# Layer 1's query stage with VectorE in written order, and the scaling of the queries behind the sums of both halves

## The chip, the core and the metric

The kernel runs on one core of one Trainium2 chip. The metric is the device time of one execution in microseconds; lower is better. The time before is 1675.03 us, the median of three runs (1675.02 to 1677.68).

The profile calls the engines PE (TensorE, the matmuls; PEld is its weight load), DVE (VectorE), ACT (ScalarE), POOL (GpSimd) and SP (SyncE, which issues nearly all DMAs here).

## What is computed

Two layers of a transformer-like backbone over 1024 latent tokens and 256 context tokens, model width 1024, fp32. Layer 0 is grouped-query attention, layer 1 multi-head latent attention with 16 heads. Only layer 1's queries matter here. Cut to them, the reference is:

```python
def q_heads(q_a, n):
    q = (rms_norm(q_a, p["q_a_norm"]) @ p["w_q_b"]).reshape(B, n, 16, 64 + 32)
    q = rms_norm(q, p["q_norm"])
    return jnp.split(q, [64], axis=-1)

kv_a, k_r, q_a, g = jnp.split(h @ p["w_in"], cuts, axis=-1)   # q_a: 384 columns, g: 1024
q_nope, q_rope = q_heads(q_a, S)
q_rope = apply_axial_rope(q_rope, cos, sin)
...
y = (o.reshape(B, S, 1024) * jax.nn.silu(g)) @ p["w_out"]
```

So each token's 384 query latents are normalised, expanded to 16 heads of 96, normalised per head, and the last 32 of each head are rotated.

## The kernel before

**Precision by splitting.** Every fp32 matrix operand is held as two parts, a high one (`wa`, `hh`, `qah`, `th`) and the rest (`wb`, `hl`, `qal`, `tl`). ACT copies out the high part, DVE or POOL subtracts it from the source (`split` in line 87 and 88; the weights in lines 158 and 137). A product is three matmuls: high by high, high by low, low by high (`mm3`, lines 94 to 96).

**The query stage.** It goes over 8 tiles of 128 tokens, in two passes. Its steps for a tile:

- `q_compress`: 24 matmuls against the input projection (384 columns), the sum of squares on ACT (L1733), the root (`rstd_of`: a multiply-add on DVE in L118, a power on POOL in L120), the scaled latents `qan` on DVE (L1736). First pass only.
- `q_latent`: three transposes on PE, the split into `qah` and `qal` (L87, L88), and their store to DRAM for the second pass (there `q_fetch` loads them).
- `q_expand`: 8 heads per pass, worked on in two halves of 4 heads (`q4`). A half is 9 matmuls of 128x384 into an `mm` buffer of PSUM, the squares on ACT (L1768), and then on DVE the sum per head (`qss`, L1770), the multiply-add of the root (`q_ms`, L118), the products with the gain and cosine table (`t`, L1775) and with the gain and sine table (two instructions `qt`, L1780). POOL takes the power (`q_rs`, L120) and adds `qt` into `t` (L1782). Last, DVE scales `t` by the root (L1783).
- `gate`: in some tiles a slice of the gate projection, 24 matmuls of 128x512, a tanh on ACT (L305) and a product on DVE (`gth`, L306), stored by SP.
- `q_store`: for each half three transposes on PE into a `tp` buffer (L1793), the split into `th` and `tl` (L87, L88), and two stores on SP (`q1h`, `q1l`, L1798).

There are four `mm` buffers and four `tp` buffers in PSUM. The tiles `th` and `tl` have two buffers each. Squares, products and gate slices share eight buffers in SBUF (tag `w512`).

**The order of the work.** `staged` writes the steps skewed: in round t it writes compress of tile t, latents of t - 1, expand of t - 3, the gate slice that belongs to t - 4, and the store of t - 6 (second pass: fetch of t, expand of t - 1, gate of t - 2, store of t - 3). The written order is not the order that runs. The framework puts each engine's instructions in an order at build time, by estimates of its own, and may take a later instruction ahead of an earlier one. Inside `with in_order(engine)` (line 82, which is the framework's manual schedule for one engine) that engine's instructions keep the written order. The key/value stage before has such a block for DVE (line 1621), and its `kv_expand` already holds the first half's scaling until the second half's sum is written. The query stage has none. The loads and splits of weights (`load_weight`, L137, L154, L158) are written before, between and behind the two passes, and stand in no block: between the passes the second half of the query expansion (`wqb`) and the second gate weight (`wg1`).

Behind the query stage come the other gate slices, and from the fifth of them on the attention's first row maxima (L402), whose operands `KH`, `QH` and `QR` SP loads from what the key/value and query stages stored.

Of the kernel before, what the change touches and what calls it, by code (L numbers as in the profile page):

```python
# [25 lines left out]
TL = NL // P  # L26
# [11 lines left out]
def hybrid_kernel(ctx: ExitStack, tc: tile.TileContext, ins: dict, out: bass.AP):  # L38
# [43 lines left out]
    def in_order(engine):  # L82

        return tc.manual_schedule(engines={engine})
# [5 lines left out]
    def mm3(ps, lh, ll, rh, rl, ks, first=True, last=True, between=None):  # L90

        ks = list(ks)
        for i, k in enumerate(ks):
            pe.matmul(ps, lhsT=lh(k), rhs=rh(k), start=first and i == 0, stop=False)  # L94
            pe.matmul(ps, lhsT=lh(k), rhs=rl(k), start=False, stop=False)  # L95
            pe.matmul(ps, lhsT=ll(k), rhs=rh(k), start=False, stop=last and i == len(ks) - 1)  # L96
            if between is not None:
                between(i)

    def staged(items, *stages):  # L100

        items = list(items)
        held = {}
        for t in range(len(items) + len(stages) - 1):
            for j, stage in enumerate(stages):
                i = t - j
                if 0 <= i < len(items):
                    held[i] = stage(items[i], held.get(i))
# [5 lines left out]
    def rstd_of(small, ss, n, tag):  # L114

        w = ss.shape[-1]
        ms = small.tile([P, w], F32, name=tag + "_ms", tag=tag + "_ms")
        dve.tensor_scalar(ms, ss, 1.0 / n, EPS, op0=ALU.mult, op1=ALU.add)  # L118
        rs = small.tile([P, w], F32, name=tag + "_rs", tag=tag + "_rs")
        pool.tensor_tensor(rs, ms, mhalf[:, :w], op=ALU.pow)  # L120
        return rs
# [17 lines left out]
    def load_weight(w, kt, c0, cols, share=2, slot=None, todo=None):  # L139
        a, b = slot or ring_pair()  # L140
        pitch = -(-cols // 64) * 64
        wh, wl = (t[:, : kt * pitch].rearrange("p (k n) -> p k n", n=pitch)[:, :, :cols] for t in (a, b))
        src = w[:, c0:c0 + cols].rearrange("(k p) n -> p k n", p=P)
        wid = min(cols, 1024)
        step = max(1, 1024 // cols)
        for k in range(0, kt, step):
            for c in range(0, cols, wid):
                n = min(step, kt - k)

                def piece(k=k, n=n, c=c):  # L150
                    r = rawp.tile([P, 1024], F32, name="wraw", tag="wraw")
                    rv = r[:, : n * wid].rearrange("p (k n) -> p k n", n=wid)
                    ks, cs = slice(k, k + n), slice(c, c + wid)
                    sp.dma_start(rv, src[:, ks, cs])  # L154

                    def parts(share=share):
                        for j in range(n):
                            act.copy(wh[:, k + j, cs], rv[:, j, :])  # L158
                            sub_any(wl[:, k + j, cs], rv[:, j, :], raw(wh[:, k + j, cs]), share)

                    return parts

                if todo is None:
                    piece()()
                else:
                    todo.append(piece)
        return wh, wl
# [126 lines left out]
    def gate_slice(l, c, m, s0, n, w, hT, ps_mm, wk, between={}):  # L294

        hh, hl = hT[0 if s0 < NL else 1]
        hs = slice(s0 % NL, s0 % NL + n)
        ms = slice(m * P, (m + 1) * P)
        ps = ps_mm.tile([P, 512], F32, name="mm", tag="mm")
        for k0 in range(0, KT, KT // 2):  # L300
            between.get(k0, lambda: None)()
            mm3(ps[:, :n], lambda k: w[0][:, k, ms], lambda k: w[1][:, k, ms],
                lambda k: hh[:, k, hs], lambda k: hl[:, k, hs], range(k0, k0 + KT // 2), k0 == 0, k0 + KT // 2 == KT)
        th = wk.tile([P, 512], F32, name="gth", tag="w512")
        act.activation(th[:, :n], ps[:, :n], AF.Tanh, scale=0.5)  # L305
        dve.scalar_tensor_tensor(th[:, :n], th[:, :n], 1.0, ps[:, :n], op0=ALU.add, op1=ALU.mult)  # L306
        sp.dma_start(sgd[l][4 * c + m, :, s0:s0 + n], th[:, :n])
# [1400 lines left out]
    with ExitStack() as st:  # L1708
# [49 lines left out]

        def q_expand(tt, c, w, lat):
            qah, qal = lat  # L1760
            held = []
            for q4 in range(2):
                ns = slice(384 * q4, 384 * q4 + 384)
                ps = ps_mm.tile([P, 512], F32, name="mm", tag="mm")
                mm3(ps[:, :384], lambda k: qah[:, k, :], lambda k: qal[:, k, :],
                    lambda k: w[0][:, k, ns], lambda k: w[1][:, k, ns], range(3))
                sq = wk.tile([P, 512], F32, name="sq", tag="w512")
                act.activation(sq[:, :384], ps[:, :384], AF.Square)  # L1768
                ss = small.tile([P, 4], F32, name="qss", tag="qss")
                dve.reduce_sum(ss, sq[:, :384].rearrange("p (h d) -> p h d", d=96), axis=AX.X)  # L1770
                rs = rstd_of(small, ss, 96, "q")
                pv = ps[:, :384].rearrange("p (h d) -> p h d", d=96)
                t1 = wk.tile([P, 512], F32, name="t1", tag="w512")
                t1v = t1[:, :384].rearrange("p (h d) -> p h d", d=96)
                dve.tensor_tensor(t1v, pv, cwq[:, tt, :].unsqueeze(1).broadcast_to([P, 4, 96]), op=ALU.mult)  # L1775
                t2 = small.tile([P, 4, 2, 2, 8], F32, name="qt2", tag="qt2")
                p5 = pv[:, :, 64:96].rearrange("p h (a s d) -> p h a s d", a=2, s=2)
                sv = swq[:, tt, :].rearrange("p (a s d) -> p a s d", a=2, s=2)
                for s_ in range(2):
                    dve.tensor_tensor(t2[:, :, :, s_, :], p5[:, :, :, 1 - s_, :],  # L1780
                                      sv[:, :, s_, :].unsqueeze(1).broadcast_to([P, 4, 2, 8]), op=ALU.mult)
                pool.tensor_add(t1v[:, :, 64:96], t1v[:, :, 64:96], t2.rearrange("p h a s d -> p h (a s d)"))  # L1782
                dve.tensor_tensor(t1v, t1v, rs.unsqueeze(2).broadcast_to([P, 4, 96]), op=ALU.mult)  # L1783
                held.append(t1)
            return held

        def q_store(tt, c, held):
            cs = slice(tt * P, (tt + 1) * P)
            for q4 in range(2):
                rows = slice(3 * (2 * c + q4), 3 * (2 * c + q4) + 3)  # L1790
                tp = ps_tp.tile([P, 512], F32, name="tp", tag="tp")
                for j in range(3):
                    pe.transpose(tp[:, j * P:(j + 1) * P], held[q4][:, j * P:(j + 1) * P], ident)  # L1793
                th = sg2.tile([P, 4, P], F32R, name="th", tag="th")
                tl = sg2.tile([P, 4, P], F32R, name="tl", tag="tl")
                split(th[:, :3], tl[:, :3], tp[:, :384].rearrange("p (a n) -> p a n", n=P))
                for dst, src in ((q1h, th), (q1l, tl)):
                    sp.dma_start(dst.rearrange("h d n -> (h d) n").rearrange("(a p) n -> a p n", p=P)[rows, :, cs].rearrange("a p n -> p a n"),  # L1798
                                 raw(src[:, :3]))
# [6 lines left out]
        def expand(c):  # L1806
            return lambda tt, lat: q_expand(tt, c, wqb[c], lat)

        def store(c):
            return lambda tt, held: q_store(tt, c, held)  # L1810

        def gate(plan):
            def fn(tt, held):
                for _ in range(plan[tt]):
                    gate_slice(1, 0, *todo_g.pop(0), 512, wg, hT, ps_mm, wk)
                return held
            return fn

        todo_g = list(slices)
        staged(range(TL), q_compress, q_latent, later, expand(0), gate((0, 0, 0, 0, 0, 1, 1, 1)), later, store(0))  # L1820
        wqb.append(load_weight(ins["l1_w_q_b"], 3, 768, 768))
        wg1 = load_weight(w_in1, KT, 1184, 512)
        staged(range(TL), q_fetch, expand(1), gate((0, 1, 0, 1, 0, 1, 1, 1)), store(1))
    stQ.close()
    stT.close()
    at.open_early(stE)
# [86 lines left out]
```

## Time and profile before

| | |
|---|---|
| Median of three runs | 1675.03 us |
| The profiled execution | 1679.43 us, span 1677.6 us |
| PE busy | 1643.1 us |
| DVE busy | 1047.3 us |
| POOL busy | 950.0 us |
| ACT busy | 640.9 us |
| First and last product of L1775 start | 990.3 and 1110.3 us |

How to read it: the span goes from the first to the last instruction of one execution; the 1.83 us beyond it lie around it. A row of the timeline gives the start in us from the span's start, the busy time in us, engine, line, operation, the tile written and the tiles read with their shapes, how many instructions were merged into the row, and in brackets how long the engine had been idle before it, and what ended that. Rows of the view of waits give who waited for whom, and then the total in us, how often, and the longest. In the names of engines a `q` stands for the sequencer that issues DMAs.

The two passes of the query stage lie between about 968 and 1117 us. In it the three transposes of L1793 belong to a half of a stored tile, 18 matmuls of 128x384 to an expanded tile, 24 of 128x512 to a gate slice.

### The profile page before, as it was taken

The page shows a single profiled execution, that of the slowest core. Times are in us where ns is not written, and L with a number is a line of the kernel's source. Part 1 is how long each engine was busy: PE and PEld are TensorE (multiplying, and loading weights), DVE is VectorE, ACT ScalarE, POOL GpSimd, SP SyncE. Part 2 cuts the span into 40 slices and gives each one's busy share as a digit, 9 for nine tenths or more (in the row PEclk, how much of TensorE's full clock was granted, in tenths as well). Part 3 has the DMA queues.
Part 4 walks back from the last instruction along what each step waited for, and adds up shares of the span by engine and source line. Part 5 has one row for each costly group of instructions (what it writes and reads, how often), then busy time and mean ns, then how long its engine had stood idle before and what let it go on. Part 6 is the DMA issues. An engine that isn't in the chain of part 4 may idle for free. (4 is left out here: it accounts for less than half of the span.)

```text
span 1677.6 us, 27271 instructions
## 1 busy us (share of the span) xinstructions
PE 1643.1 (98%) x10236; PEld 1192.1 (71%) x10236; DVE 1047.3 (62%) x1660; ACT 640.9 (38%) x944; POOL 950.0 (57%) x624
## 2 busy tenths in 40 slices
PE   8999999999999999999999999999999999999998
PEld 5776768885555555558878898887766767667587
DVE  3674553357788877625675657755777777677231
ACT  3652222224455544432234533341434534434310
POOL 2673431118899898842235645350768778777521
PEclk9999999999999999999999999999999999999999
DMA  8547856532252432256424766767466565653451
GB/s 287 199 123 248 254 167 201 154 98 58 76 145 70 122 82 77 56 150 200 141 71 136 231 186 180 220 203 195 119 133 148 125 137 119 133 134 79 122 175 69
DMA packets 221116, 244.21 MB, mean 146 GB/s; under 512 B 23160, under 2 KB 160616, under 8 KB 220984
## 3 DMA queue, kind: packets, MB, share of 16 engines
q1 hardware_dynamic: 220560, 242.36, 51.8%
q8 instruction: 81, 1.33, 0.3%
q14 instruction: 51, 0.42, 0.1%
q10 hardware_dynamic: 424, 0.11, 0.0%
HBM read 168.62 MB, written 73.63 MB: 144 GB/s over the span
## 5 line engine op out<-in xcount | busy, mean ns | idle before, releaser
L567 ACT ACTIVATE p<-st 128x1024 f32<-128x1024 f32 x328 | 335.9, 1027 | 156.9 <-PE st L560 142.3
L601 POOL TENSOR_TENSOR acp<-acp,p 128x1024 f32<-128x1024 f32 x128 | 305.3, 2385 | 8.3 <-ACT p L567 0.4
L404 DVE TENSOR_REDUCE m<-mx 128x1 f32<-128x512 f32 x256 | 175.7, 691 | 95.6 <-PE mx L402 89.9
L445 DVE TENSOR_REDUCE m<-mx 128x1 f32<-128x1024 f32 x128 | 150.5, 1220 | 68.6 <-PE mx L436 68.1
L601 POOL TENSOR_TENSOR acp<-p 128x1024 f32<-128x1024 f32 x34 | 81.5, 2400 | 177.3 <-ACT p L567 177.2
L617 PE MATMUL avt<-p,v 128*64 128x512 f32 x672 | 152.5, 598 | 0.6 <-DVE crow L476 0.3
L601 POOL TENSOR_TENSOR acp<-acp,acd 128x1024 f32<-128x1024 f32 x60 | 141.9, 2365 | 14.3 <-DVE acd L587 11.0
L587 DVE TENSOR_REDUCE acd<-p 128x512 f32<-128x1024 f32 x124 | 144.7, 1220 | 6.9 <-ACT p L567 6.9
L617 PE MATMUL av<-p,v 128*64 128x512 f32 x640 | 141.1, 595 | 0.0
L137 POOL TENSOR_TENSOR wb<-wraw,wa 128x512 fp32r<-128x512 f32 (+3 forms) x65 | 86.9, 1351 | 84.2 <-ACT wa L158 83.4
L94 PE MATMUL mm<-wa,hh 128*128 128x512 f32 (+2 forms) x336 | 128.4, 382 | 1.0 <-ACT hh L974 1.0
L96 PE MATMUL mm<-wa,hl 128*128 128x512 f32 (+2 forms) x336 | 122.6, 365 | 1.5 <-DVE hl L977 1.5
L560 PE MATMUL st<-QH,KH 64*128 64x512 f32 x320 | 122.5, 407 | 0.6 <-DVE gth L306 0.5
L95 PE MATMUL mm<-wb,hh 128*128 128x512 f32 (+2 forms) x336 | 122.2, 364 | 0.0
L560 PE MATMUL st<-QH,KL 64*128 64x512 f32 x320 | 117.9, 391 | 0.0
L560 PE MATMUL st<-QL,KH 64*128 64x512 f32 x320 | 117.5, 390 | 0.0
L94 PE MATMUL y<-wa,oh 128*128 128x512 f32 (+1 forms) x296 | 114.0, 385 | 0.6 <-ACT oh L813 0.6
L96 PE MATMUL y<-wa,ol 128*128 128x512 f32 (+1 forms) x296 | 113.4, 384 | 0.3 <-DVE ol L814 0.3
L95 PE MATMUL y<-wb,oh 128*128 128x512 f32 (+1 forms) x296 | 113.5, 383 | 0.0
L617 PEld LDWEIGHTS av<-p,v 128*64 128x64 f32 x640 | 44.4, 137 | 88.3 <-issue 87.6
L617 PEld LDWEIGHTS avt<-p,v 128*64 128x64 f32 x672 | 44.9, 136 | 86.9 <-issue 80.6
L94 PE MATMUL mm<-hh,wa 128*128 128x512 f32 (+1 forms) x264 | 103.1, 390 | 1.2 <-DVE qt L1780 1.2
(247 smaller groups left out, 4025.6 us busy)
## 6 DMA issues: line engine op xcount, KB each, us to landing
mraw<-in_l_w_mod SPq DMA_DIRECT2D x64, 256.0 KB
wraw<-in_l_w_in SPq DMA_DIRECT2D x28, 512.0 KB
KH<-k1h SPq DMA_DIRECT2D x32, 320.0 KB
KL<-k1l SPq DMA_DIRECT2D x32, 320.0 KB
rb<-rrow SPq DMA_DIRECT2D x72, 128.0 KB
mraw<-in_l_w_mod SPq DMA_DIRECT2D x16, 512.0 KB
QA<-q0h SPq DMA_DIRECT2D x32, 256.0 KB
wraw<-in_l_w_out SPq DMA_DIRECT2D x16, 512.0 KB
```

The source lines that it names most:

```text
L94: pe.matmul(ps, lhsT=lh(k), rhs=rh(k), start=first and i == 0, stop=False)
L95: pe.matmul(ps, lhsT=lh(k), rhs=rl(k), start=False, stop=False)
L96: pe.matmul(ps, lhsT=ll(k), rhs=rh(k), start=False, stop=last and i == len(ks) - 1)
L137: eng.tensor_sub(lo, a, b)
L404: dve.reduce_max(s["m"][:, i, n:n + 1], held["m"], axis=AX.X)
L445: dve.reduce_max(s["m"][:, i, 0:1], m, axis=AX.X)
L560: pe.matmul(ps[:, n * 512:(n + 1) * 512], lhsT=lh, rhs=rh, start=j == 0, stop=j == last)
L567: act.activation(p, ps, AF.Exp, scale=self.ops["scale"])
L587: dve.reduce_sum(t[:, ns], p2.rearrange("p a n -> p n a")[:, ns, :], axis=AX.X)
L601: pool.tensor_add(t, a, b)
L617: pe.matmul(s["av"][64 * n:64 * n + 64, :], lhsT=s["v"][:, kt, u["vc"]:u["vc"] + 64], rhs=p[:, n * 512:(n + 1) * 512], start=kt == kts[0], ...
```

## The change

Both calls of `staged` in the query stage are put into a block in which DVE keeps the written order, one block for each pass. In `q_expand` the scaling of a half by its root (L1783) is no longer written at the end of the half: it is held in a list, and both halves' scalings are written after both halves' sums and products. No instruction is added or taken away.

```diff
         def q_expand(tt, c, w, lat):
             qah, qal = lat
-            held = []
+            held, todo = [], []
             for q4 in range(2):
...
                 pool.tensor_add(t1v[:, :, 64:96], t1v[:, :, 64:96], t2.rearrange("p h a s d -> p h (a s d)"))
+                held.append(t1)
+                todo.append((t1v, rs))
+            for t1v, rs in todo:
                 dve.tensor_tensor(t1v, t1v, rs.unsqueeze(2).broadcast_to([P, 4, 96]), op=ALU.mult)
-                held.append(t1)
             return held
...
         todo_g = list(slices)
-        staged(range(TL), q_compress, q_latent, later, expand(0), gate((0, 0, 0, 0, 0, 1, 1, 1)), later, store(0))
+        with in_order(mybir.EngineType.DVE):
+            staged(range(TL), q_compress, q_latent, later, expand(0), gate((0, 0, 0, 0, 0, 1, 1, 1)), later, store(0))
         wqb.append(load_weight(ins["l1_w_q_b"], 3, 768, 768))
         wg1 = load_weight(w_in1, KT, 1184, 512)
-        staged(range(TL), q_fetch, expand(1), gate((0, 1, 0, 1, 0, 1, 1, 1)), store(1))
+        with in_order(mybir.EngineType.DVE):
+            staged(range(TL), q_fetch, expand(1), gate((0, 1, 0, 1, 0, 1, 1, 1)), store(1))
```

## The prediction, made before the result was known

> **What bounds the kernel now.** I read the page first, then the waits of PE from 955 to 1140 us, where the query stage lies, then the timelines of PE, DVE, POOL, ACT and SP around each of those waits, and the chain of waits last.
>
> ```profile
> span 1677.6 us, 27271 instructions
> PE 1643.1 (98%) x10236; PEld 1192.1 (71%) x10236; DVE 1047.3 (62%) x1660; ACT 640.9 (38%) x944; POOL 950.0 (57%) x624
> ```
>
> PE is the bound: it is busy in all but 34.5 of 1677.6 us. The change takes no matmul away, so it can only win idle time of PE. The waits of PE in this stretch (who waited, for whom: us in total, times, longest):
>
> ```profile
> PE tp L1612 <- DVE kn L1576: 2.8, 2, 2.0
> PE tp L1793 <- DVE tl L88: 2.7, 3, 1.5
> PE tp L1793 <- POOL wb L137: 1.5, 1, 1.5
> PE mm L94 <- DVE qt L1780: 1.2, 1, 1.2
> ```
>
> The first row is the end of the key/value stage, ahead of the change. The other three are the query stage: 2.7 + 1.5 + 1.2 = 5.4 us, and this is the most that can be won there. The timeline of PE has four of these five waits as rows, with the wait in brackets:
>
> ```profile
> 1027.99 0.52 PE L1793 MATMUL tp<-ident,t 128*128 128x128 f32 x3 [1.55 <-DVE tl L88]
> 1056.59 0.52 PE L1793 MATMUL tp<-ident,t 128*128 128x128 f32 x3 [0.81 <-DVE tl L88]
> 1067.05 0.47 PE L94 MATMUL mm<-hh,wa 128*128 128x512 f32 x1 [1.18 <-DVE qt L1780]
> 1116.01 0.98 PE L1793 MATMUL tp<-ident,t 128*128 128x128 f32 x6 [1.46 <-POOL wb L137]
> ```
>
> The fifth is 2.70 - 1.55 - 0.81 = 0.34 us just before the second. Exactly, the sum is 1.55 + 1.15 + 1.18 + 1.46 = 5.34 us. All five are waits for a buffer that DVE empties: a transpose needs one of four `tp` buffers, freed by the subtraction `tl` (L88), and a product needs one of four `mm` buffers, freed by `qt` (L1780).
>
> **What the change does to DVE's order.** One tile of queries (the fifth, tt = 4 of the first pass) on DVE:
>
> ```profile
> 1021.10 2.63 DVE L137 TENSOR_TENSOR wb<-wraw,wa 128x768 fp32r<-128x768 f32 x1
> 1023.66 0.54 DVE L1770 TENSOR_REDUCE qss<-sq 128x4 f32<-128x384 f32 x1
> 1024.23 0.17 DVE L118 TENSOR_SCALAR q_ms<-qss 128x4 f32<-128x4 f32 x1
> 1024.31 0.55 DVE L1775 TENSOR_TENSOR t<-mm,cwq 128x384 f32<-128x384 f32 x1
> 1024.78 0.35 DVE L1780 TENSOR_TENSOR qt<-mm,swq 128x64 f32<-128x64 f32 x2
> 1025.04 0.54 DVE L1770 TENSOR_REDUCE qss<-sq 128x4 f32<-128x384 f32 x1
> 1026.02 0.56 DVE L1783 TENSOR_TENSOR t<-t,q_rs 128x384 f32<-128x384 f32 x1 [0.44 <-POOL t L1782]
> ...
> 1027.30 0.55 DVE L88 TENSOR_TENSOR tl<-tp,th 128x384 fp32r<-128x384 f32 x1
> 1028.28 0.56 DVE L1783 TENSOR_TENSOR t<-t,q_rs 128x384 f32<-128x384 f32 x1 [0.43 <-POOL t L1782]
> 1028.75 0.55 DVE L88 TENSOR_TENSOR tl<-tp,th 128x384 fp32r<-128x384 f32 x1
> ```
>
> and on POOL:
>
> ```profile
> 1024.55 1.01 POOL L120 TENSOR_TENSOR q_rs<-q_ms,mhalf 128x4 f32<-128x4 f32 x1 [1.63 <-DVE q_ms L118]
> 1025.53 0.46 POOL L1782 TENSOR_TENSOR t<-t,qt 128x128 f32<-128x128 f32 x1
> ```
>
> Before, the first half's scaling (L1783) stands in front of the second half's `q_ms`, `t` and `qt`, and waits for POOL; so POOL's second power waits for `q_ms`, too. A `tl` of an older tile fills the second half's wait. The change puts both scalings behind both halves, and the two `tl`, which are written after the whole tile, behind both scalings. Worked out on these rows: up to 1025.04 nothing moves. The second `q_ms` comes 0.57 us after its sum (1024.23 - 1023.66), at 1025.61, its `t` at 1025.69, its `qt` at 1026.16, and the first scaling 0.26 us on (1025.04 - 1024.78), at 1026.42. POOL's second power would start 0.32 us after `q_ms` (1024.55 - 1024.23) but has to let the first addition end (1025.53 + 0.46 = 1025.99); the addition follows it by 0.98 us, at 1026.97, and ends at 1027.43. The second scaling starts there, 0.03 us on (1026.02 - 1025.99), at 1027.46 where it stood at 1028.28: 0.82 us earlier. The first `tl` follows 0.47 us later (1028.75 - 1028.28), at 1027.93 where it stood at 1027.30: 0.63 us later. The second comes at 1028.40, 0.35 us earlier. Everything DVE has to do in the next tile moves by these 0.35 us, tile after tile.
>
> **The terms.** (1) The wait at 1027.99 ends with the first `tl`, which DVE now has queued behind both scalings: +0.63 us. The weight split at 1021.10, which made DVE late, is outside the ordered blocks and I leave it where it is.
>
> (2) The waits of 0.34 and 0.81. The chain of waits has
>
> ```profile
> 1050.58 0.94 DVE tl L88 x2
> 1052.68 3.11 DMA q1l<-tl
> ```
>
> The two `tl` at 1050.58 are stored, and the next `tl` into their buffers waits until the store has landed, 3.11 us. That store was late because DVE was. Up to 1050 DVE works through this tile and three more; at 0.35 us each, or 0.82 where no `tl` had filled the wait, the stores go out 1.4 (4 x 0.35) to 3.3 us (4 x 0.82) earlier, and 1.15 suffice: -1.15 us. The other end is 0, if the store then stands longer in a busy queue.
>
> (3) The wait of 1.18 ends with a `qt` that no longer has a scaling in front of it, but PE, too, comes there 1.15 us earlier, and `tl` instructions that wait for stores still lie among the second pass's first tiles. Between 0 and -1.18 I take the middle, -0.59.
>
> (4) The wait of 1.46 is put down to a split on POOL, but this transpose needs a `tp` buffer, and the `tl` that frees one ends at nearly the same time (1115.87, the first of two):
>
> ```profile
> 1104.32 1.64 DVE L1783 TENSOR_TENSOR t<-t,q_rs 128x384 f32<-128x384 f32 x1 [1.36 <-POOL t L1782]
> 1105.88 4.06 DVE L137 TENSOR_TENSOR wb<-wraw,wa 128x512 fp32r<-128x512 f32 x3
> 1112.37 0.59 ACT L305 ACTIVATE gth<-mm 128x512 f32<-128x512 f32 x1
> 1114.72 0.68 DVE L306 SCALAR_TENSOR_TENSOR gth<-gth,mm 128x512 f32<-128x512 f32 x1
> 1115.32 1.01 DVE L88 TENSOR_TENSOR tl<-tp,th 128x384 fp32r<-128x384 f32 x2
> ```
>
> DVE waits 1.36 us for the last tile's first scaling, needs 1.64 for it, splits weights for 4.06, and only then comes to the second half. With the scaling moved back the splits can begin up to 3.0 us (1.36 + 1.64) earlier. Ahead of `tl` stays the gate's product, which waits for ACT until 1112.96 (1112.37 + 0.59); with 0.68 us for the product and 0.55 for `tl` that is 1114.2, and PE is done with its earlier work at 1116.01 - 1.46 = 1114.55. So -1.46; the other end is 0, if splits still stand ahead of `tl`.
>
> Sum: 0.63 - 1.15 - 0.59 - 1.46 = -2.57 us. The profiled execution took 1679.43 us (span 1677.6 and 1.83 around it), 4.4 above the median of 1675.03; I carry the difference over: 1676.9 there, **1672.5** for the median.
>
> **A port.** The scaling reads two SBUF tensors and now runs beside POOL's second power. Its nearest rows:
>
> ```profile
> 1039.57 0.95 DVE L137 TENSOR_TENSOR wb<-wraw,wa 128x768 fp32r<-128x768 f32 x1
> 1040.06 0.77 POOL L1782 TENSOR_TENSOR t<-t,qt 128x128 f32<-128x128 f32 x1
> ```
>
> The same split took 2.63 at 1021.10, where POOL split weights too, and 0.95 here, beside a power and an addition; the addition paid 0.31 (0.77 - 0.46). So I price the scaling's company at 0 on DVE; the far end is 1.08 (1.64 - 0.56), which would lie on term (1) alone and make the sum -1.49, 1673.5. [...]
>
> **Rivals.** *All of it goes.* If the new order also moves the split of 2.63 us away from in front of this tile, the first `tl` comes before PE needs it, and all 5.34 us go: 1669.7. For it: that split stands where DVE was waiting, and these places change. Against it: ACT makes its input just before, and the tile's first half waits for nothing new.
>
> *Slower: the two ordered blocks become one row.* Then the second pass's first sum cannot pass the first pass's last `tl`. In the trace this `tl` runs at 1066.09 and the sum at 1058.19:
>
> ```profile
> 1058.19 0.55 DVE L1770 TENSOR_REDUCE qss<-sq 128x4 f32<-128x384 f32 x1 [1.76 <-ACT sq L1768]
> 1066.09 0.56 DVE L88 TENSOR_TENSOR tl<-tp,th 128x384 fp32r<-128x384 f32 x1
> 968.02 0.52 PE L96 MATMUL mm<-wa,hl 128*128 128x384 f32 x1
> 972.82 0.34 PE L96 MATMUL mm<-wa,hl 128*128 128x384 f32 x1
> 972.99 0.34 PE L94 MATMUL mm<-wa,hh 128*128 128x384 f32 x1
> ```
>
> The sum would start at 1066.65 and its `qt` end 1.47 us on (1024.78 + 0.35 - 1023.66), at 1068.1. PE can fill four `mm` buffers, 36 matmuls of 0.17 us from about 1056.9, to 1063.1, and would wait 5.0 us instead of 1.18: +3.8. The clock adds to it: behind the waits of 2.0 and 0.8 us at the key/value stage's end, 15 matmuls stand 0.32 us apart (968.02 to 972.82) instead of 0.17, which is 2.2 us. With terms (1), (2) and (4): 3.8 + 2.2 + 0.63 - 1.15 - 1.46 = +4.0, 1679.0. It decides at whether a later block may start while an earlier one has instructions left. Against it, on DVE, the border of two earlier such blocks (the key/value stage's order, and layer 0's last projection):
>
> ```profile
> 865.20 0.15 DVE L1539 TENSOR_SCALAR kvms<-kvss 128x1 f32<-128x1 f32 x1 [0.21 <-ACT sq L1536]
> 867.26 0.68 DVE L137 TENSOR_TENSOR hl<-hmod,hh 128x512 fp32r<-128x512 f32 x1
> ```
>
> The later block's `kvms` runs ahead of the earlier block's `hl`. [...]
>
> *Given back at the hand-over.* The first maxima of the attention begin as soon as their loads are there:
>
> ```profile
> 1138.73 0.50 PE L402 MATMUL mx<-KH,QH 64*128 64x512 f32 x2
> ```
>
> SP issues these loads (`KH`, `QH`, `QR`) behind the last tiles' stores. If the stores do not move with PE, PE waits at 1138.73 for what it won: about 1675. Against it: the stores hang on the same `tl`.
>
> **How the numbers follow.** A measurement of this kernel can tell about 0.2%, 3.35 us, from no change. Forecast as summed, 0.30, of which 0.05 may pass the bound; the port's price on top of it, 0.08; all of it goes, 0.33; given back, or an order that hardly differs from the one before (the scheduler already kept nearly the written order), 0.09; slower, 0.20: 0.12 for the joined blocks, 0.08 for orders on PE and SP that come out worse by as much. So faster 0.38, within 0.42, slower 0.20. The forecast's own range is 1669.7 (all waits) to 1676.7 (only term (1), with the port's 1.08). Eight in ten reach from 1669.0 to 1679.5, which takes in the joined blocks.
>
> **What would show it.** DVE's wait of L1783 for POOL happens 16 times, once a tile, with about 0.57 us each (1027.46 - 1026.42 - 0.47); the wait near 1028 is about 2.2 us; those near 1056 and 1114 are gone. A wait of PE of 3 us or more in the stage, or one at the first maxima, would make it wrong.

## The result, and the profile after

The changed kernel takes 1671.85 us (median of 19 executions, 1668.51 to 1675.58), the kernel before 1674.31 us (19 executions beside them). The ratio is 0.9984, with a 95% interval of 0.9976 to 0.9992: a gain of some 2.5 us, which is clear of the noise and smaller than the 0.2% that the prediction takes as its bound. The forecast was 1672.5 us, 2.53 below the time that it started from.

The page of the changed kernel's profiled execution (1672.5 us) begins with

```profile
span 1670.7 us, 27270 instructions
PE 1636.6 (98%) x10236; PEld 1187.6 (71%) x10236; DVE 1051.1 (63%) x1660; ACT 640.6 (38%) x944; POOL 950.8 (57%) x624
```

This span is 6.9 us shorter than that of before, but 3.28 us of it stand there before the change acts: the third tile's latents are transposed (L1743) at 987.19 us before and at 983.91 after, and up to there PE and DVE run the same order. So the two traces are compared from that mark to the attention's first maxima (L402), called the stage below: 151.54 us before (1138.73 - 987.19), 148.15 after (1132.06 - 983.91), a difference of 3.39. PE's waits from 955 to 1140 us, to be held against the four rows of before:

```profile
PE tp L1612 <- DVE kn L1576: 2.5, 2, 1.7
PE tp L1743 <- DVE qa_ms L118: 2.5, 1, 2.5
PE tp L1795 <- DVE tl L88: 2.1, 1, 2.1
PE mm L94 <- DVE qt L1780: 0.4, 1, 0.4
```

The second lies ahead of the mark. Of the 5.34 us inside the stage 2.49 are left, in two rows of PE's timeline (the transposes are L1795 now, the scaling L1786):

```profile
1025.58 0.52 PE L1795 MATMUL tp<-ident,t 128*128 128x128 f32 x3 [2.07 <-DVE tl L88]
1062.11 0.47 PE L94 MATMUL mm<-hh,wa 128*128 128x512 f32 x1 [0.42 <-DVE qt L1780]
```

Start of the same work in both traces, and what each stretch gave:

| Mark | before | after | shift | stretch |
|---|---|---|---|---|
| third latents | 987.19 | 983.91 | -3.28 | |
| gate slice behind the fifth tile's wait | 1031.47 | 1028.72 | -2.75 | +0.53 |
| transposes behind the waits near 1056 | 1065.28 | 1061.19 | -4.09 | -1.34 |
| gate slice that waited for `qt` | 1067.05 | 1062.11 | -4.94 | -0.85 |
| gate slices behind the last transposes | 1116.75 | 1110.08 | -6.67 | -1.73 |
| first maxima | 1138.73 | 1132.06 | -6.67 | 0.00 |

DVE's waits for POOL at the scaling, before (L1783) and after (L1786):

```profile
DVE t L1783 <- POOL t L1782: 24.1, 31, 2.2
```

```profile
DVE t L1786 <- POOL t L1782: 8.6, 16, 2.2
```

One wait a tile instead of two; without the longest they are (8.6 - 2.2) / 15 = 0.43 us each. The fifth tile on DVE, after:

```profile
1017.74 0.95 DVE L137 TENSOR_TENSOR wb<-wraw,wa 128x768 fp32r<-128x768 f32 x1
1018.60 0.55 DVE L1770 TENSOR_REDUCE qss<-sq 128x4 f32<-128x384 f32 x1
1019.18 1.22 DVE L118 TENSOR_SCALAR q_ms<-qss 128x4 f32<-128x4 f32 x1
...
1021.50 0.94 DVE L137 TENSOR_TENSOR wb<-wraw,wa 128x768 fp32r<-128x768 f32 x1
1022.37 0.42 DVE L118 TENSOR_SCALAR q_ms<-qss 128x4 f32<-128x4 f32 x1
...
1023.44 0.54 DVE L1786 TENSOR_TENSOR t<-t,q_rs 128x384 f32<-128x384 f32 x1
1024.41 0.56 DVE L1786 TENSOR_TENSOR t<-t,q_rs 128x384 f32<-128x384 f32 x1 [0.43 <-POOL t L1782]
1024.89 1.01 DVE L88 TENSOR_TENSOR tl<-tp,th 128x384 fp32r<-128x384 f32 x2
```

Both `tl` stand behind both scalings, as written. The split of 2.63 us is gone; two splits of 0.95 and 0.94 have come into this tile, and the first `q_ms` takes 1.22 us where 0.17 is its usual time. Beside it, on POOL:

```profile
1017.79 2.58 POOL L137 TENSOR_TENSOR wb<-wraw,wa 128x768 fp32r<-128x768 f32 x1 [1.09 <-ACT wa L158]
1020.54 1.01 POOL L120 TENSOR_TENSOR q_rs<-q_ms,mhalf 128x4 f32<-128x4 f32 x1 [0.17 <-DVE q_ms L118]
```

### The profile page after: what moved, and what is told of

Read it like the earlier page. It is cut to its first block, busy times and chain, and to the rows that moved or that the text cites. A ratio compares the mean times of both kernels' runs of the same rounds, so it can differ in the third digit from the quotient of the medians.

```text
span 1670.7 us, 27270 instructions
## 1 busy us (share of the span) xinstructions
PE 1636.6 (98%) x10236; PEld 1187.6 (71%) x10236; DVE 1051.1 (63%) x1660; ACT 640.6 (38%) x944; POOL 950.8 (57%) x624
```

## The experiments

Theory A: the deferral wins the time, since DVE no longer waits for POOL inside a tile. Rival B: the written order wins it. For the wait of 2.07 us, A has the older tile's `tl` behind both scalings (term 1), the rival the weight splits. All runs, with PE's waits inside the stage in order of time, the stage, the stage less these waits, the median and the ratio to the kernel before (medians of 1674.33, 1674.15 and 1674.12 us beside the three groups of runs), with its interval:

| Kernel | waits | stage | less waits | median | ratio |
|---|---|---|---|---|---|
| before | 1.55, 0.34, 0.81, 1.18, 1.46 | 151.54 | 146.20 | | |
| changed | 2.07, 0.42 | 148.15 | 145.66 | 1671.85 | 0.9984 (0.9976 to 0.9992) |
| changed, again | 2.05 | 147.71 | 145.66 | 1670.89 | 0.9980 (0.9971 to 0.9989) |
| order alone | 3.01, 0.93, 0.52, 3.95 | 159.12 | 150.71 | 1680.99 | 1.0045 (1.0032 to 1.0057) |
| deferral alone | 2.23, 1.48, 1.13 | 151.14 | 146.30 | 1674.40 | 1.0001 (0.9992 to 1.0009) |
| order in first pass | 2.08, 0.40, 1.13 | 151.16 | 147.55 | 1673.68 | 0.9994 (0.9985 to 1.0003) |
| order in second pass | 2.23, 0.42 | 150.05 | 147.40 | 1673.53 | 0.9994 (0.9984 to 1.0003) |
| the same, again | 1.83, 2.15 | 150.07 | 146.09 | 1673.73 | one execution |
| `wqb` split on POOL | 3.31, 0.29 | 150.70 | 147.10 | 1673.66 | 1.0001 (0.9991 to 1.0011) |
| both split on POOL | 3.33, 1.17 | 150.58 | 146.08 | 1677.19 | 1.0024 (1.0014 to 1.0034) |
| the same, one block | 3.35, 3.45, 1.17 | 158.33 | 150.36 | 1682.54 | 1.0055 (1.0041 to 1.0069) |
| `tl` between | 1.43, 0.34 | 147.61 | 145.84 | 1671.35 | 0.9986 (0.9977 to 0.9996) |
| and `wqb` split on DVE | 0.45, 0.35 | 146.61 | 145.81 | 1669.20 | 0.9977 (0.9964 to 0.9989) |
| and `wqb` loaded later | 0.30 | 146.40 | 146.10 | 1668.88 | 0.9969 (0.9957 to 0.9981) |

The column of the stage less its waits splits the kernels: 145.7 to 146.3 where PE kept its clock in the stage, 147.1 and more where it did not (below).

**Order alone.** Each scaling back at the end of its half:

```
                 held.append(t1)
-                todo.append((t1v, rs))
-            for t1v, rs in todo:
                 dve.tensor_tensor(t1v, t1v, rs.unsqueeze(2).broadcast_to([P, 4, 96]), op=ALU.mult)
```

> Both passes on VectorE in written order, each scaling at the end of its own half as before the change. Measured from the third latents' first transpose to the attention's first maxima (151.54 us in the kernel before, 148.15 in the changed one). Theory A (the deferral wins the time, because VectorE no longer waits for GpSimd inside a tile): with the order kept and no deferral VectorE waits for GpSimd 32 times, and no subtraction tl of an older tile may fill the first of the two waits; a tile takes VectorE about 0.9 us longer than in the changed kernel, so the waits near 1028, 1056, 1067 and 1116 stay or grow: 151.5 to 155 us, the kernel the same as before or up to 3.5 us slower. Rival B (the written order wins the time, because it keeps tl from being put behind splits and sums): most of the 3.4 us stays won, 148 to 149.5 us.

B falls: the order by itself costs 6.7 us (1680.99 - 1674.33). DVE's row for the scaling (L1784 there):

```profile
DVE t L1784 <- POOL t L1782: 28.4, 32, 1.6
```

It stands 0.9 us at each of the 32 scalings, and nothing may pass. The stage (159.12 us) came out beyond A's range, too. Only 3.07 of the 7.58 us more than before are waits (8.41 against 5.34); behind the waits of 3.01 and 3.95 us the granted clock is 0.85 from 1028 to 1036 us and 0.77 from 1115 to 1130.

**Deferral alone**, both ordered blocks taken out:

```
-        with in_order(mybir.EngineType.DVE):
+        if True:
```

> Scalings behind both halves, VectorE's order left to the scheduler. From the third latents' first transpose to the attention's first maxima: 151.54 us before, 148.15 after the change. Theory A (the deferral wins the time): terms 2 and 4, some 3.1 us, stay won, 148 to 149 us, and the ratio to the kernel before is 0.998. Rival B (the written order wins it): the scheduler is free to put a weight split in front of a tl again, 150.5 to 152 us, ratio 0.9995 to 1.000.

A as it was put falls as well: the ratio is 1.0001. Of the old waits the two near 1056 are gone, those at `qt` and at the last transposes stay. The last tile on DVE shows why:

```profile
1100.31 1.64 DVE L1786 TENSOR_TENSOR t<-t,q_rs 128x384 f32<-128x384 f32 x1 [1.36 <-POOL t L1782]
1101.87 4.07 DVE L137 TENSOR_TENSOR wb<-wraw,wa 128x512 fp32r<-128x512 f32 x3
1105.86 0.54 DVE L1770 TENSOR_REDUCE qss<-sq 128x4 f32<-128x384 f32 x1
1108.57 1.63 DVE L1786 TENSOR_TENSOR t<-t,q_rs 128x384 f32<-128x384 f32 x1 [1.37 <-POOL t L1782]
```

The first scaling is written behind the second sum (L1770) and runs ahead of it, with the same 1.36 and 1.64 us as before the change: without the block the framework undoes the deferral here. In the changed kernel the same tile reads

```profile
1098.64 0.69 DVE L137 TENSOR_TENSOR wb<-wraw,wa 128x512 fp32r<-128x512 f32 x1 [0.74 <-ACT wa L158]
1099.67 3.06 DVE L137 TENSOR_TENSOR wb<-wraw,wa 128x512 fp32r<-128x512 f32 x2 [0.34 <-ACT wa L158]
1102.65 0.54 DVE L1770 TENSOR_REDUCE qss<-sq 128x4 f32<-128x384 f32 x1
...
1104.55 0.54 DVE L1786 TENSOR_TENSOR t<-t,q_rs 128x384 f32<-128x384 f32 x1
1105.53 0.56 DVE L1786 TENSOR_TENSOR t<-t,q_rs 128x384 f32<-128x384 f32 x1 [0.44 <-POOL t L1782]
```

**Order in one pass**, the deferral in both; the second pass's block taken out, then the first's:

> Scalings behind both halves in both passes, written order in the first pass alone. Both theories share term 1 and 2 here (first pass: about -0.8 us net, gained by 1061 us). If the second pass's order matters, the wait near 1116 (1.46 us before, gone after the change) comes back and the span from the third latents' transposes to the first maxima is 149.5 to 150.5 us; if the deferral alone does it, the wait stays away and the span is 148 to 148.5 us.

> Scalings behind both halves in both passes, written order in the second pass alone. If the first pass's order causes term 1 (the wait near 1028 grew by 0.5 us in the changed kernel because the first tl is queued behind both scalings), it is 1.5 us or less here, and the span from the third latents' transposes to the first maxima 147.5 to 148 us; if terms 2 and 3 need the order, their waits (0.34, 0.81 and 1.18 us before) come back and the span is 149.5 to 150.5 us.

The last wait (1.13) comes back exactly where the second pass has no block, so term 4 hangs on that block. The wait at the fifth tile is not shorter without the first pass's block (2.23 us), against what was expected there. DVE's rows show why: the framework puts both `tl` behind both scalings here without a block, too, so this kernel doesn't test their order:

```profile
1023.36 0.56 DVE L1786 TENSOR_TENSOR t<-t,q_rs 128x384 f32<-128x384 f32 x1 [1.33 <-POOL t L1782]
1023.84 1.01 DVE L88 TENSOR_TENSOR tl<-tp,th 128x384 fp32r<-128x384 f32 x2
```

By waits alone the second kernel should have won 2.7 us (5.34 - 2.65) and won 0.8 (1674.33 - 1673.53); its trace has a lower clock around the wait (the row of the windows: stretch, length, PE busy, clock, DMA share, GB/s):

```profile
1020.00:1028.00 8.00, 5.77 (x28) 0.81 0.98 278
```

A second trace of the same kernel:

> The kernel with the written order in the second pass alone, for a second trace. If the lower clock behind the wait near 1025 us is chance of the execution, it may be 1.00 here; if it belongs to this order, it is again 0.81 to 0.85 between 1020 and 1028 us. By waits alone this kernel would win 2.7 us against the kernel before (2.23 and 0.42 instead of 5.34).

```profile
1020.00:1028.00 8.00, 6.17 (x38) 1.00 1.00 284
```

So this order does not force the lower clock. Whether it was chance this pair can't show, since the wait ahead was shorter here, 1.83 us (POOL's second power took 1.01 us where it had taken 1.45). This trace also shows what ends the wait at `qt`, on DVE and then on PE:

```profile
1062.24 0.56 DVE L88 TENSOR_TENSOR tl<-tp,th 128x384 fp32r<-128x384 f32 x1 [2.12 <-DMA q1l<-tl]
1062.71 0.34 DVE L1780 TENSOR_TENSOR qt<-mm,swq 128x64 f32<-128x64 f32 x2
```

```profile
1063.20 0.47 PE L94 MATMUL mm<-hh,wa 128*128 128x512 f32 x1 [2.15 <-DVE qt L1780]
```

A `tl` that waits for an earlier store to land stands in front of `qt`. With this order the wait was 0.42 in one execution and 2.15 in another.

**The changed kernel again**, for a second trace:

> The changed kernel unaltered, for a second trace of it. In the traces so far a wait of 2.07 to 3.35 us at the fifth tile's transposes was followed by a lower granted clock in five kernels (about 1.9 us more for the next 40 matmuls) and not in three, and the five are those that also show a lower clock between 955 and 980 us. If that is chance of the execution, this trace may show the wait of 2.07 with a clock below 0.95 between 1020 and 1036 us; if it belongs to the kernel's order, the clock is 1.00 again. Theory A (term 1) and the others expect the same waits as before, 2.07 and 0.42, and a ratio of 0.998 to 0.999.

The wait is 2.05 us, the clock 1.00 again; the wait at `qt` is gone altogether. The supposed link has an exception: this trace has a clock of 0.83 from 955 to 965 us and none below 1.00 at the fifth tile.

**The splits of the second half's query matrix on POOL**:

```
-        wqb.append(load_weight(ins["l1_w_q_b"], 3, 768, 768))
+        wqb.append(load_weight(ins["l1_w_q_b"], 3, 768, 768, 0))
```

> The changed kernel with all weight splits of the second half's query matrix on GpSimd, so that VectorE has none in the first pass. Theory A (the wait of 2.07 us at the fifth tile's transposes is the older tile's tl queued behind both scalings): the splits took VectorE 0.95 and 0.94 us of that tile, outside the ordered instructions; without them the wait shrinks by at most their share, to 1.0 us or more. Rival (the splits alone make VectorE late there): the wait goes altogether and the span from the third latents' first transpose to the first maxima falls from 148.15 to about 146. A cost on the other side: GpSimd is later with its powers and additions, and the second pass's first products wait for weights.

Both expectations fail: the wait grows to 3.31 us. What decides is the cost on GpSimd's side that the expectation names last. POOL holds the power back behind two splits, and the addition behind a third:

```profile
1016.17 3.65 POOL L137 TENSOR_TENSOR wb<-wraw,wa 128x768 fp32r<-128x768 f32 x2 [0.36 <-ACT wa L158]
1019.77 1.02 POOL L120 TENSOR_TENSOR q_rs<-q_ms,mhalf 128x4 f32<-128x4 f32 x1
1020.75 1.84 POOL L137 TENSOR_TENSOR wb<-wraw,wa 128x768 fp32r<-128x768 f32 x1
1022.53 0.47 POOL L1782 TENSOR_TENSOR t<-t,qt 128x128 f32<-128x128 f32 x1
```

**Both weights' splits on POOL, and then one block in place of two.** The control has `0` for both loads; the other moves them inside the first block and drops the second `with`.

> As the changed kernel, with the splits of both weight matrices that are loaded behind the first pass on GpSimd. It is the control for the joined order below: 146 to 149 us from the third latents' first transpose to the first maxima if GpSimd has the time for them, more if the gate's products wait for weights.

> As the control with all those splits on GpSimd, and one written order on VectorE through both passes instead of two. The rival of the joined blocks priced this at +3.8 us of waiting for TensorE where the passes meet (a wait of 5.0 us instead of 1.18), and 2.2 us for a dropped clock behind it: 4 to 6 us longer than the control if the price was right. If VectorE's order at the border costs less than that (the last tl of the first pass may come earlier than in the kernel before), the difference is under 1.5 us.

The control's stage is longer than expected, 150.58 us, by the same wait of 3.3 us at the fifth tile. One block costs 5.35 us on top of it (1682.54 - 1677.19; the two ratios' intervals stand apart), within the 4 to 6 that the price of the joined blocks gives. The traces differ by 7.75 in the stage: 3.47 in waits, the rest by the clock, which is 0.82 already at the fifth tile, ahead of the border, and 0.89 from 1060 to 1075 us. DVE at the border of the passes:

```profile
1058.22 0.56 DVE L88 TENSOR_TENSOR tl<-tp,th 128x384 fp32r<-128x384 f32 x1 [2.70 <-DMA q1l<-tl]
1059.94 0.56 DVE L88 TENSOR_TENSOR tl<-tp,th 128x384 fp32r<-128x384 f32 x1 [1.16 <-DMA q1l<-tl]
1061.54 0.56 DVE L88 TENSOR_TENSOR tl<-tp,th 128x384 fp32r<-128x384 f32 x1 [1.05 <-PE mm L95]
1063.02 0.56 DVE L88 TENSOR_TENSOR tl<-tp,th 128x384 fp32r<-128x384 f32 x1 [0.92 <-DMA q1l<-tl]
1063.49 0.54 DVE L1770 TENSOR_REDUCE qss<-sq 128x4 f32<-128x384 f32 x1
```

The second pass's first sum stands behind the first pass's last `tl`, and PE waits 3.45 us (the profile puts it down to "issue"). In the changed kernel this sum runs at 1054.11 and that `tl` at 1061.14: two blocks do not act as one.

The control shows another rival at work. Its stage is shorter than that of before, and it is 3 us slower all the same. PE has this row at the hand-over:

```profile
1134.54 0.46 PE L402 MATMUL mx<-KH,QH 64*128 64x512 f32 x1 [0.97 <-DMA QH<-q1h]
```

The maxima wait for queries that were stored late, and the clock behind that is 0.83 from 1132 to 1138 us and 0.88 from 1138 to 1144. From the first maxima to the end it takes 541.9 us (1675.0 - 1133.07), the changed kernel 538.6 (1670.7 - 1132.06), and so does every other kernel here to within 0.3 us, but for the one with one block (542.4).

**`tl` between the scalings.** The second half's scaling is written behind the older tile's first `tl` (or ahead of the next tile's sums, where there is none):

```
+            scale_q(*todo[0])
+            late.append(todo[1])
...
                 split(th[:, :3], tl[:, :3], tp[:, :384].rearrange("p (a n) -> p a n", n=P))
+                if q4 == 0:
+                    scale_late()
```

> The changed kernel with the second half's scaling written behind the first tl of the older tile, so that this tl runs in VectorE's wait for GpSimd. Theory A (term 1: the first tl stands behind both scalings): the wait of 2.07 us near 1026 falls by about 0.5 us to 1.0, to 1.0 to 1.6 us, and the span from the third latents' first transpose to the first maxima from 148.15 to 147.1 to 147.7 us. Rival (the weight splits make VectorE late there, and the order of the two instructions doesn't matter): the wait stays at 1.9 to 2.1 us and the span at 148.0 to 148.3.

The wait falls by 0.64 us to 1.43, as A has it. Of this 0.34 is given back at the last tile, where the second `tl` now has a scaling ahead of it, so the stage (147.61) is hardly shorter than in the changed kernel's second trace, and the ratios don't tell the two apart.

**And the three `wqb` splits on DVE** (`1` for the share of the load):

> The kernel with tl between the two scalings, and all three weight splits of the second half's query matrix on VectorE. So far the wait at the fifth tile grew from 2.07 to 3.31 us when these splits went to GpSimd. If GpSimd's splits are what makes that tile late (its power comes behind a split of 2.58 us, and beside it VectorE's mean took 1.22 us instead of 0.17), the wait of 1.43 us falls by about 1 us, to 0.2 to 0.8, and the kernel is 0.5 to 1 us faster than with tl between alone. If VectorE's own time counts (one more split of 0.95 us in that tile), the wait stays at 1.3 to 1.6 us or grows.

With three splits of 0.95 us on DVE instead of two, and none on POOL, the wait falls from 1.43 to 0.45. The first `q_ms` is short again:

```profile
1017.61 0.16 DVE L118 TENSOR_SCALAR q_ms<-qss 128x4 f32<-128x4 f32 x1
```

**And the load of `wqb` written later**, in the sixth tile's gate step:

```
             def fn(tt, held):
+                if tt == 5 and len(wqb) == 1:
+                    wqb.append(load_weight(ins["l1_w_q_b"], 3, 768, 768))
                 for _ in range(plan[tt]):
...
-        wqb.append(load_weight(ins["l1_w_q_b"], 3, 768, 768))
```

> The kernel with tl between the two scalings, and the load of the second half's query matrix written into the sixth tile's gate step, so that its splits on VectorE and GpSimd come where the gate's products give both engines time. If the splits, on whichever engine, make the fifth tile late, the wait of 1.43 us goes (0 to 0.4 us) and the kernel is 1 to 1.5 us faster than with tl between alone, the fastest of all; if the load now comes too late, the first products of the second pass wait by about the same amount. If the chain inside a tile alone makes it, the wait stays at 1.4.

The wait is gone, with the two splits that DVE had in that tile. The call now stands inside the first block, so DVE runs them where they are written:

```profile
1030.57 2.08 DVE L137 TENSOR_TENSOR wb<-wraw,wa 128x768 fp32r<-128x768 f32 x2
```

The block binds DVE alone. Against the expectation, POOL's split stays in the fifth tile:

```profile
1015.68 1.83 POOL L137 TENSOR_TENSOR wb<-wraw,wa 128x768 fp32r<-128x768 f32 x1 [1.09 <-ACT wa L158]
1016.61 0.92 DVE L118 TENSOR_SCALAR q_ms<-qss 128x4 f32<-128x4 f32 x1
```

ACT's copies of this weight stay there as well, 32.2 us behind the mark here (1014.02 - 981.81) and with `tl` between alone (1016.06 - 983.83). So it is DVE's splits whose leaving ends the wait. The kernel has the lowest median of all, 1668.88 us, 2.0 below the changed kernel in the same group of runs (1670.89). The two ratios' intervals overlap a little, though, and from the kernel ahead of it in the table (1669.20) the medians don't tell it apart. The stage is 1.3 us shorter than in the changed kernel (147.71 - 146.40).

## Why the prediction was right

**Term 1** (+0.63) was right in size, +0.53, and in mechanism: moving the `tl` ahead of one scaling took 0.64 off. What failed is the sentence that the split at 1021.10 stays where it is. It left, and two others came. That this changed the wait by so little (1.43 us without the order's 0.64, 1.55 before) is luck, and without it the sum for this term would have been off. The remaining 1.43 us belong to weight splits on both engines and not to the order of `tl`: 0.98 went when POOL's split left the tile, though DVE got one more, and all of it when DVE's two left and POOL's stayed.

**Term 2** (-1.15) came as -1.34, and 1.15 of it are the two waits. The two `tl` of the prediction's chain start at 1050.49 on DVE's timeline before and at 1045.31 after. That is 5.18 us earlier, or 1.90 beyond the 3.28 from ahead of the mark, inside the 1.4 to 3.3 that the prediction works out. The next two wait for no store any more:

```profile
1045.31 1.01 DVE L88 TENSOR_TENSOR tl<-tp,th 128x384 fp32r<-128x384 f32 x2
1051.13 1.01 DVE L88 TENSOR_TENSOR tl<-tp,th 128x384 fp32r<-128x384 f32 x2
```

The waits are gone wherever the scalings are deferred, with and without blocks. The kernel with the order alone doesn't show them either, but there PE comes 3.1 us later to this place, so it tells nothing.

**Term 3** (-0.59, the middle of its range) came as -0.85. Its size is set by when a store lands, as the text had it; executions of kernels with the deferral and a block (the joined one aside) gave between 0 and 0.42, and once 2.15, above the 1.18 of before. That the middle came so near is luck: the changed kernel's own wait was 0.42 in one trace and 0 in the other, where the term would be -1.18.

**Term 4** (-1.46) came as -1.73, with the wait gone: the splits begin before the scaling, as worked out. But the prediction put this to the deferral, and it needs the second pass's block.

In sum -3.39 in the two traces, where the five waits account for 2.85 (5.34 - 2.49). The other 0.54 is in no wait of PE that the profile shows, and stays open; it is within what the stage less its waits differs by among the traces at full clock (145.66 to 146.30). The median moved by 2.46, the second group's by 3.23 (1674.12 - 1670.89).

**The rivals.** *All of it goes* was right that the split of 2.63 leaves this tile and wrong that nothing else comes. *Joined blocks* was well priced as a mechanism (3.45 us of waiting, where 5.0 was worked out, instead of none, and a clock of 0.89 behind it; 5.35 in the medians), but its condition doesn't hold. *Given back at the hand-over* doesn't happen here: no wait at 1132.06, and the stretch of 0.00 above; it happens when both weights' splits go to POOL. *The port's price* is 0 for the scaling beside POOL's power, where it takes 0.54 to 0.56 us. Beside a split on POOL it isn't: in the kernel before, a scaling of the last tile takes 1.64 us (1104.32, 0.08 us behind the start of POOL's splits at 1104.24); in the changed kernel's second trace one of the last tile takes 1.63 us, and no wait of PE follows. VectorE is held up at an instruction with one small input, too: `q_ms` takes 1.22 us beside a split on POOL and 0.16 without one. No run here shows what makes the two engines wait for each other; "port" is the prediction's name for it.

What the prediction did not see is that neither half of the edit wins anything alone that the medians show. It worked out the order that the text asks for, and took for granted that DVE would run it.

## What to carry to other kernels

Where a framework reorders, an edit of the written order and the block that enforces it are one change: the block alone freezes waits that the framework was filling (+6.7 us, with a clock of 0.85 and 0.77 behind two of them), the edit alone is partly undone (a ratio of 1.0001). Before settling for the better order, look at what else runs in the tile that waits: here weight splits that feed products that start some 30 us later (1051 against 1021 us) cost more than the order of the two subtractions did (1.43 us of that wait against 0.64). Compare traces from a mark behind which the orders differ, and take a second trace where the clock or a landing DMA differs between executions (here 0.81 and 1.00 at the fifth tile, and waits of 0.42 and 2.15 us at `qt`, in two executions of one kernel).

## What the runs showed of the hardware that was not expected

**The length of a short wait did not decide the clock behind it.** At the fifth tile waits of 1.83, 2.05, 2.07, 2.23 and 3.33 us left the granted clock at 1.00, and waits of 2.08, 2.23, 3.31 and 3.35 were followed by 0.81 to 0.85 from 1020 to 1028 us. Between the control's first maxima a wait of 0.97 us was followed by 0.83. Of the nine traces with 2.05 us or more at the fifth tile, eight have a lower clock there exactly when they have one between 955 and 980 us, and the changed kernel's second trace is the exception. So it may hang on the execution; what decides it stays open. By the column of the stage less its waits one drop costs about 0.8 to 1.9 us (147.10 to 147.55 against 145.66 to 146.30); the prediction had 2.2. The forecast has no term for a drop behind the wait that it puts at 2.2 us, and the changed kernel's two traces show none.

**One drop was free.** In the kernel before, the clock is 0.77 from 965 to 980 us and PE doesn't wait at the first latents; after, it is 1.00 there and PE waits 2.47 us for DVE:

```profile
977.48 0.52 PE L1743 MATMUL tp<-ident,qan 128*128 128x128 f32 x3 [2.47 <-DVE qa_ms L118]
```

The shift between the two traces hardly changes over this place (-3.53 us where the 62 products ahead of these transposes start, 967.55 before and 964.02 after; -3.28 at the third latents): a slower PE only used up time that it would have waited.

**Some long instructions here are waits for the other engine.** The `q_ms` of 1.22 us in the changed kernel ends at 1020.40, and POOL's split beside it at 1020.37 (1017.79 + 2.58). The one of 0.42 ends at 1022.79, POOL's addition at 1022.76. In the last kernel the one of 0.92 ends at 1017.53, the split at 1017.51. The rows show it the other way round, too. That addition, which starts 0.02 us behind a split of 0.94 on DVE (1021.50), takes 1.24 us where 0.46 is usual. By these ends the one that starts first runs first, and the other's busy time holds its wait. POOL's power did not hold DVE up like this: the scaling at 1023.44 takes its usual 0.54 us inside a power that lasts from 1022.94 to 1023.95. So the split of 2.63 us in the kernel before, which starts 0.02 us behind one of 1.84 on POOL, is no measure of DVE's work: with all three `wqb` splits on DVE and none on POOL each takes 0.95.
